# The second half of x arrives transposed; TensorE spreads the inverse roots

## The chip, the cores and the metric

One core of a Trainium2 chip runs the kernel. The metric is the time of one execution on the device in microseconds (us), as the median of several runs. A profile of one execution shows where the time goes. TensorE multiplies matrices into PSUM, VectorE and ScalarE work on SBUF and PSUM, GpSimd (POOL) on SBUF, and SyncE (SP) issues the DMAs.

## The reference

One layer of a streaming encoder, for a prompt of 2048 frames and 64 further frames of a running stream, with D = 1024:

```python
def rmsnorm(x, g=None):
    y = xf * lax.rsqrt(jnp.mean(xf * xf, axis=-1, keepdims=True) + EPS)
    return y * g

h = rmsnorm(x, norm_g) @ w_in
qa, ka, va, za, qb, kb, vb, zb, ga, gb = jnp.split(h, _split_points(), axis=-1)
# branch A: differential attention on qa, ka, va; branch B: retention on qb, kb, vb
m = ga * (oa @ w_oa) + gb * (ob @ w_ob)
return x + m @ w_out
```

What is changed concerns the first step alone: x is normalised frame by frame (one inverse root for each frame, one gain norm_g for each of the 1024 channels), and the product with w_in needs it with the channels on the partitions.

## The kernel before

**Precision.** A product in fp32 is made of three fast ones: each operand is split into a high part (rounded to fp32r) and a low part (the rest), and hi·hi, hi·lo and lo·hi are added up in PSUM. So x is kept as `xh` and `xl`, the weights as `wh` and `wl`. Every 128-channel chunk of a product is three matmuls (`mm_group`, L484 to L501; the matmuls are L493).

**Two halves.** The 2048 frames are worked off in two halves of 1024, the 64 sample frames with the first. `xh` and `xl` hold one half, in two segments of 512 frames (the second with 64 more in the first half). For each half all columns of w_in pass by, in blocks: va, ka, qa (frames on the output's partitions, `natural`, L576, with the finishes `fin_va` L685 and `fin_qk` L605), later qb, kb, za, zb, ga, gb (`transposed`, L738, with `fin_t` L754). The last block of the first half is the second part of gb. When its last product with a segment has been issued, that segment is free (`seg_free`, L751), and the second half's frames are put into it.

**How the second half of x is made.** When the first half is at its last block, `x_prep(1)` (L254) begins to load eight tiles of 128 frames into buffers of the tag `row`, eight of 128x1024 that attention shares. `x_norm` (L352) makes each tile's inverse root: squares with their sum on ScalarE (L321), log and exponential there (L323, L324), a correction on VectorE (L330 to L338); then VectorE scales the tile by the root and by the gain, which was broadcast over the partitions by a DMA (L347, `gn`). `x_tile` (L364) then transposes the tile on TensorE, four 128x128 blocks into one bank of PSUM (`tp`) and four into another (`pv`), both L376; ScalarE copies a bank to `xh` (L383), and VectorE takes the difference to `xl` (L384).

**What comes next.** The first block of the second half is va again, in groups of two tiles: 48 matmuls of 128x256. Its finish `fin_va` copies the result on ScalarE to `thi` (L698) and to `raw` (L700) and takes the rest on VectorE to `tlo` (L702), and three DMAs store them.

**What sets the order.** The code is a set of generators with priorities. A loop (L86) runs the one with the best priority that can go on, and keeps a clock of its own for each engine, moved by assumed costs (`P`, `A`, `V`, `G`, `ld`, L119 to L139). A generator that must wait yields the time at which it wants to go on. So the order in which each engine gets its instructions is worked out when the program is built; on the chip every engine runs its list in that order and waits on semaphores. The loop decides what stands ahead of what in a list, and not when it runs. All DMAs go through SP's list.

## Time and profile before

| | |
|---|---|
| median of 3 runs | 2009.26 us (2008.01 to 2015.51) |
| the profiled execution's own time | 2009.56 us |
| its span, first to last instruction | 2007.8 us |
| mean granted TensorE clock | 0.997 |
| GpSimd waiting for ScalarE's weight copies (wl L465 <- wh L455) | 620.2 us in total |
| TensorE's longest wait for another engine | 3.0 us |

Lines of the profile read as follows. In the order of time: start, duration, engine, line, operation, output<-inputs, shape, count, and in brackets the idle time ahead of it with what ended it. In the groups: busy time of the group and the mean duration of one in ns, then idle time ahead of its instructions. PE is TensorE, DVE VectorE, ACT ScalarE, SPq the DMA issues of SP. Matmuls overlap in the pipeline, so the step from one start to the next, and not the duration, is the time that one takes in a stream. In a table by stretches each engine has its busy time, PEclk is the granted clock (1.00 is full speed).

### The profile page before, as it was taken

What the parts mean: (1) busy time and instruction counts of PE and PEld (TensorE: products, weight loads), DVE (VectorE), ACT (ScalarE), POOL (GpSimd) and SP (SyncE); (2) the same over time, 40 slices, a digit from 0 to 9 for tenths busy, and PEclk for the clock granted to TensorE, in tenths of its full rate; (3) what the DMA queues carried; (4) which work ended last, traced back from release to release, by engine and by line L of the source; (5) the groups of instructions that cost most, each with busy time, mean ns of one, the idle gap of its engine ahead of it and who ended that gap; (6) DMA issues with size and microseconds to landing.
All of it is one profiled execution on the core that took longest, in us unless ns stands there. A gap on an engine that the chain in (4) does not pass through costs nothing. (4 is left out here: it accounts for less than half of the span.)

```text
span 2007.8 us, 34354 instructions
## 1 busy us (share of the span) xinstructions
PE 1988.0 (99%) x12412; PEld 1784.0 (89%) x12412; DVE 991.3 (49%) x2661; ACT 955.6 (48%) x2096; POOL 420.3 (21%) x387
## 2 busy tenths in 40 slices
PE   9999999999999999999999999999999989999999
PEld 7778999999998999999999888888888878889997
DVE  5452666553331421446856555635653365444442
ACT  6432776654442433536665656635654553333320
POOL 2310211211111212221211111122112442222210
PEclk9999999999999999999999999999999999999999
DMA  7647454344565563563352352553234674444431
GB/s 247 199 145 178 135 157 123 109 141 141 157 169 130 146 185 92 180 200 111 117 160 80 91 154 66 142 171 95 64 97 128 197 224 153 149 140 138 137 94 59
DMA packets 330268, 280.96 MB, mean 140 GB/s; under 512 B 64689, under 2 KB 296113, under 8 KB 330098
## 3 DMA queue, kind: packets, MB, share of 16 engines
q1 hardware_dynamic: 330098, 278.77, 47.1%
q8 instruction: 98, 1.61, 0.3%
q14 instruction: 72, 0.59, 0.1%
HBM read 187.19 MB, written 91.49 MB: 139 GB/s over the span
## 5 line engine op out<-in xcount | busy, mean ns | idle before, releaser
L493 PE MATMUL mm<-xh,wh 128*128 128x512 f32 (+2 forms) x1280 | 461.2, 360 | 0.0
L493 PE MATMUL mm<-xh,wl 128*128 128x512 f32 (+2 forms) x1280 | 451.7, 353 | 0.0
L493 PE MATMUL mm<-xl,wh 128*128 128x512 f32 (+2 forms) x1280 | 450.9, 352 | 0.0
L465 POOL TENSOR_TENSOR wl<-ws,wh 128x512 fp32r<-128x512 f32 x189 | 250.8, 1339 | 903.6 <-ACT wh L455 620.2
L493 PE MATMUL mm<-wh,xh 128*128 128x256 f32 (+3 forms) x864 | 272.0, 315 | 0.3 <-DVE tlo L702 0.3
L493 PEld LDWEIGHTS mm<-xh,wl 128*128 128x128 f32 x1280 | 240.9, 188 | 32.0
L493 PEld LDWEIGHTS mm<-xh,wh 128*128 128x128 f32 x1280 | 241.2, 188 | 29.6 <-issue 0.2
L493 PEld LDWEIGHTS mm<-xl,wh 128*128 128x128 f32 x1280 | 241.4, 189 | 29.1
L493 PE MATMUL mm<-wh,xl 128*128 128x256 f32 (+3 forms) x864 | 267.0, 309 | 0.1
L493 PE MATMUL mm<-wl,xh 128*128 128x256 f32 (+3 forms) x864 | 266.6, 309 | 0.0
L759 ACT COPY ev<-mm 128x512 f32<-128x512 f32 x140 | 71.6, 511 | 242.0 <-PE mm L493 217.8
L493 PEld LDWEIGHTS mm<-wh,xh 128*128 128x128 f32 (+1 forms) x864 | 162.2, 188 | 11.4 <-ACT xh L383 0.5
L493 PEld LDWEIGHTS mm<-wl,xh 128*128 128x128 f32 (+1 forms) x864 | 162.4, 188 | 10.6
L493 PEld LDWEIGHTS mm<-wh,xl 128*128 128x128 f32 (+1 forms) x864 | 162.2, 188 | 10.7 <-DVE xl L384 0.8
L1055 DVE TENSOR_TENSOR atl<-at,ath 128x512 fp32r<-128x512 f32 (+1 forms) x144 | 93.8, 660 | 139.9 <-ACT ath L1053 139.8
L972 ACT ACTIVATE row<-row,a_mx 128x1024 f32<-128x1024 f32 (+7 forms) x160 | 153.5, 962 | 16.8 <-DVE a_mx L952 16.7
L942 DVE CUSTOM_DVE_ANT_0 row<-s,dfar 128x512 f32<-128x512 f32 (+2 forms) x192 | 117.9, 632 | 74.8 <-PE s L934 73.6
L455 ACT CAST wh<-ws 128x512 fp32r<-128x512 f32 x192 | 116.5, 618 | 41.4 <-PE mm L493 28.0
L1053 ACT CAST ath<-at 128x512 fp32r<-128x512 f32 (+1 forms) x144 | 79.6, 563 | 99.2 <-PE at L1040 96.7
L933 PE MATMUL s<-K,q 128*128 128x512 f32 (+3 forms) x320 | 120.3, 381 | 2.5 <-DVE a_acc L942 2.5
L934 PE MATMUL s<-K,q 128*128 128x512 f32 (+3 forms) x320 | 115.5, 362 | 0.8 <-DMA q<-qT 0.8
L993 DVE SCALAR_TENSOR_TENSOR row<-row,a_w 128x1024 f32<-128x1024 f32 (+4 forms) x96 | 98.1, 1032 | 26.7 <-ACT row L990 26.4
(208 smaller groups left out, 3943.1 us busy)
## 6 DMA issues: line engine op xcount, KB each, us to landing
ws<-in_w_in_dram SPq DMA_DIRECT2D x192, 256.0 KB, 3.1
q<-qT SPq DMA_DIRECT2D x128, 128.0 KB, 3.0
V<-vN SPq DMA_DIRECT2D x24, 512.0 KB, 5.2
K<-kT SPq DMA_DIRECT2D x48, 256.0 KB, 4.4
gt<-gaT SPq DMA_DIRECT2D x64, 132.0 KB, 2.1
gt<-gbT SPq DMA_DIRECT2D x64, 132.0 KB, 2.2
xt<-in_x_prompt_dram SPq DMA_DIRECT2D x16, 512.0 KB, 6.0
kn<-in_cache_k_T_dram SPq DMA_DIRECT2D x32, 256.0 KB, 3.6
```

The costliest lines, as they stand in the source:

```text
L455: self.nc.scalar.copy(h, st)
L465: self.nc.gpsimd.tensor_sub(l, st, h.bitcast(F32))
L493: nc.tensor.matmul(ps, p, q, start=c == 0 and i == 0, stop=c == KC - 1 and i == 2)
L759: nc.scalar.copy(ev, ps)
L933: nc.tensor.matmul(ps, q1s, kk, start=True, stop=False)
L934: nc.tensor.matmul(ps, q2s, kk, start=False, stop=True)
L942: nc.vector.tensor_tensor_reduce(out=units[k0 // 1024][:, k0 % 1024:k0 % 1024 + n], in0=ps, in1=tab, scale=-SLOPES[h], scalar=3.0e38, op0= ...
L972: nc.scalar.activation(u, u, AF.Exp, bias=mx, scale=-1.0, accum_out=lp[:, k:k + 1])
L993: nc.vector.scalar_tensor_tensor(out=u0, in0=u0, scalar=w[:, 0:1], in1=u1, op0=ALU.mult, op1=ALU.add)
L1053: nc.scalar.copy(ah[:, :w], at[:, :w])
L1055: nc.vector.tensor_sub(al[:, :w], at[:, :w], ah[:, :w].bitcast(F32))
```

## The change

The host hands in `x_prompt` a second time, transposed. The kernel loads the second half of x in four pairs of tiles (256 frames): as before, to get the roots, and transposed, as two buffers of 4 chunks x 256 frames. The tiles themselves are no longer transposed. Each tile's 128 roots are put on the diagonal of a 128x128 matrix (`dg`, VectorE), and TensorE multiplies a matrix of ones (1/128; the root is multiplied by 128) by it: every partition then has all roots of the frames in PSUM. VectorE multiplies the transposed frames, chunk by chunk, by this and by the gain of the channel, which now lies on the partition (`gT`, a small load at the start). ScalarE copies the result to `xh`, VectorE takes the difference to `xl`, 1024 columns at a time. The first half of x is made as before.

```diff
+        self.gT = c("gT", [128, 8])
+        self.ld(self.gT, i["norm_g"][0].rearrange("(c p) -> p c", p=128))
...
+    def xt_load(self):
+        yield from self.take("row", 2)
+        jk, dg = self.row("xjk"), self.row("dg")
+        for p in range(4):
+            t0 = 1024 + 256 * p
+            dp = dg[:, 256 * p:256 * p + 256]
+            for u in range(2):
+                yield from self.take("row")
+                xt = self.row("xt")
+                t = self.ld(xt, self.i["x_prompt"][0, t0 + 128 * u:t0 + 128 * u + 128, :], 1 << 19)
+                self.spawn(self.xt_root(xt, jk, dp[:, 128 * u:128 * u + 128], t, p), 1, "w")
+            yield from self.take("row", 2)
+            xT = [self.row("xT") for _ in range(2)]
+            for k in range(2):
+                t = self.ld(xT[k].rearrange("p (c t) -> p c t", c=4),
+                            self.i["x_prompt_T"][512 * k:512 * k + 512, t0:t0 + 256]
+                            .rearrange("(c p) t -> p c t", p=128), 1 << 19)
+            self.xin.append([xT, t, dp, []])
+            yield self.pe
...
+    def xt_root(self, xt, jk, dg, t, p):
...
+        nc.vector.tensor_scalar(dg, self.ident, y, None, op0=ALU.mult)
...
+    def xt_pairs(self):
+        for p in range(4):
+            seg, col = p // 2, 256 * (p % 2)
...
+            rb = self.psum("tp")[:, :256]
+            for u in range(2):
+                nc.tensor.matmul(rb[:, 128 * u:128 * u + 128], self.ones, dp[:, 128 * u:128 * u + 128],
+                                 start=True, stop=True)
...
+            for k in range(2):
+                for c in range(4):
+                    xc = xT[k][:, 256 * c:256 * c + 256]
+                    nc.vector.scalar_tensor_tensor(out=xc, in0=xc, scalar=self.gT[:, 4 * k + c:4 * k + c + 1],
+                                                   in1=rb, op0=ALU.mult, op1=ALU.mult)
...
+            for k in range(2):
...
+                nc.scalar.copy(hi, xk)
+                t2 = self.A(1024, t)
+                yield t2
+                nc.vector.tensor_sub(lo, xk, hi.bitcast(F32))
+                t2 = self.V(1024, t2)
+                self.give("row", t2)
+            self.xt_ready += [t2, t2]
...
-                    self.spawn(self.x_prep(1), 1, "w")
-                    self.xt_ready = []
-                    self.spawn(self.x_tiles(8), 2, "w")
+                    self.xt_ready, self.xin = [], []
+                    self.spawn(self.xt_load(), 1, "w")
+                    self.spawn(self.xt_pairs(), 2, "w")
...
+    given["x_prompt_T"] = np.ascontiguousarray(given["x_prompt"][0].T)
```

More of the change, by code (lines that the diff above doesn't have):

```diff
@@ L39 @@
 QUANT = 6
-XFLY = (3, 5)
+XFLY = 3
 EARLY = 3
@@ L252, in x_alloc, with x_prep @@
         self.xl[seg] = xp.tile([128, KC, n], F32R, tag=f"xl{seg}", name=f"xl{seg}")
-    def x_prep(self, half):
+    def x_prep(self):
         self.xq = []
@@ L257, in x_prep @@
         self.xfly = 0
-        gn = jk = tg = None
-        if half:
-            yield from self.take("row", 2)
-            gn, jk = self.row("gn"), self.row("xjk")
-        else:
-            yield from self.take("row")
-            jk = self.row("xjk")
-        tiles = self.xtiles(half)
+        gn = tg = None
+        yield from self.take("row")
+        jk = self.row("xjk")
+        tiles = self.xtiles(0)
         left = [len(tiles)]
         for j, (src, r, seg, col) in enumerate(tiles):
-            yield lambda: self.xfly < XFLY[half] and (half > 0 or j < 2 or self.wloads >= 8)
+            yield lambda: self.xfly < XFLY and (j < 2 or self.wloads >= 8)
             self.xfly += 1
@@ L273, in x_prep @@
             tx = self.ld(xt, src, 4096 * r)
-            if j == 0 and half == 0:
+            if j == 0:
                 yield from self.take("row")
@@ L282, in x_prep @@
                 self.gz = (gz, tg)
-            elif j == 0:
-                tg = self.ld(gn, self.i["norm_g"][0].partition_broadcast(128), 1 << 19)
             self.xin.append([xt, jk, gn, tx, tg, r, seg, col, left])
-            if half:
-                self.spawn(self.x_norm(j), 1, "w")
             yield self.pe
         yield lambda: left[0] == 0
-        if half == 0:
-            self.give("s", self.dve + LAT, 2)
-        self.give("row", self.dve + LAT, 1 + half)
+        self.give("s", self.dve + LAT, 2)
@@ new lines, in x_prep @@
+        self.give("row", self.dve + LAT)
+    def xt_load(self):
+        nc = self.nc
+        yield from self.take("row", 2)
[3 more added lines that the diff above has]
+            dp = dg[:, 256 * p:256 * p + 256]
+            td = 0.0
+            for u in range(2):
+                yield from self.take("row")
+                xt = self.row("xt")
[9 more added lines that the diff above has]
+            yield self.pe
+        yield lambda: len(self.xt_ready) == 8
+        self.give("row", self.pe + LAT, 2)
@@ new lines, in xt_root @@
+    def xt_root(self, xt, jk, dg, t, p):
+        nc = self.nc
+        yield t
+        st = self.sp.tile([128, 3], F32, tag="x_st", name="x_st")
+        ss, ms, y = (st[:, k:k + 1] for k in range(3))
+        nc.scalar.activation(jk, xt, AF.Square, accum_out=ss)
+        t = self.A(1024, self.pe, 190)
+        self.give("row", t)
+        nc.scalar.activation(y, ss, AF.Ln, scale=1.0 / D, bias=self.epst)
+        nc.scalar.activation(y, y, AF.Exp, scale=-0.5)
+        self.A(1, 0, 40)
+        t2 = self.A(1, 0, 40)
+        yield t
+        nc.vector.tensor_scalar(ms, ss, 1.0 / D, EPS, op0=ALU.mult, op1=ALU.add)
+        self.V(1, t)
+        yield t2
+        nc.vector.tensor_scalar(ms, y, y, ms, op0=ALU.mult, op1=ALU.mult)
+        nc.vector.tensor_scalar(ms, ms, -0.5, 1.5, op0=ALU.mult, op1=ALU.add)
+        nc.vector.tensor_scalar(y, y, ms, 128.0, op0=ALU.mult, op1=ALU.mult)
+        nc.vector.tensor_scalar(dg, self.ident, y, None, op0=ALU.mult)
+        for _ in range(4):
+            t = self.V(40, t2)
+        self.xin[p][3].append(t)
@@ new lines, in xt_pairs @@
+    def xt_pairs(self):
+        nc = self.nc
+        for p in range(4):
+            seg, col = p // 2, 256 * (p % 2)
+            yield lambda: len(self.xin) > p and len(self.xin[p][3]) == 2
+            xT, tx, dp, ts = self.xin[p]
+            yield max(ts)
+            yield from self.take("tp")
+            rb = self.psum("tp")[:, :256]
+            for u in range(2):
+                nc.tensor.matmul(rb[:, 128 * u:128 * u + 128], self.ones, dp[:, 128 * u:128 * u + 128],
+                                 start=True, stop=True)
+                t = self.P(512)
+            if max(t, tx) > self.pe:
+                yield max(t, tx)
+            for k in range(2):
[3 more added lines that the diff above has]
+                                                   in1=rb, op0=ALU.mult, op1=ALU.mult)
+                    t = self.V(256, t)
+            self.give("tp", t)
+            if p % 2 == 0:
+                yield lambda: self.seg_free[seg] is not None
+                yield self.seg_free[seg]
+                self.seg_free[seg] = None
+                self.x_alloc(seg)
+            if t > self.pe:
+                yield t
+            for k in range(2):
+                hi = self.xh[seg][:, 4 * k:4 * k + 4, col:col + 256]
+                lo = self.xl[seg][:, 4 * k:4 * k + 4, col:col + 256]
+                xk = xT[k].rearrange("p (c t) -> p c t", c=4)
+                nc.scalar.copy(hi, xk)
+                t2 = self.A(1024, t)
+                yield t2
+                nc.vector.tensor_sub(lo, xk, hi.bitcast(F32))
+                t2 = self.V(1024, t2)
+                self.give("row", t2)
+            self.xt_ready += [t2, t2]
@@ L337, in norm_root @@
         nc.vector.tensor_scalar(ms, ms, -0.5, 1.5, op0=ALU.mult, op1=ALU.add)
-        nc.vector.tensor_scalar(y, y, ms, 128.0 if isinstance(self.xin[j][2], list) else 1.0,
-                                op0=ALU.mult, op1=ALU.mult)
+        nc.vector.tensor_scalar(y, y, ms, 128.0, op0=ALU.mult, op1=ALU.mult)
         for _ in range(3):
@@ L344, in norm_scale @@
         xt, jk, gn, tx, tg, r, seg, col, left, ss, ms, y, t, t2 = self.xin[j]
-        for k, g in enumerate(gn if isinstance(gn, list) else [gn]):
-            sl = slice(512 * k, 512 * k + g.shape[1])
+        for k, g in enumerate(gn):
+            sl = slice(512 * k, 512 * k + 512)
             self.nc.vector.scalar_tensor_tensor(out=xt[:, sl], in0=xt[:, sl], scalar=y, in1=g[:r],
@@ L350, in norm_scale, with x_tile @@
         left[0] -= 1
-    def x_norm(self, j):
-        yield self.xin[j][3]
-        self.norm_sums(j)
-        ss, ms, y, t, t2 = self.xin[j][9:]
-        yield t
-        self.norm_mean(j)
-        yield t2
-        self.norm_root(j)
-        if self.xin[0][4] > self.pe:
-            yield self.xin[0][4]
-        self.norm_scale(j)
-    def x_tile(self, j, wait=True):
+    def x_tile(self, j):
         nc = self.nc
-        yield lambda: len(self.xq) > j and self.xq[j] is not None
         xt, t, r, seg, col = self.xq[j]
-        if wait:
-            yield t
         self.until(t)
@@ L389, in x_tile @@
         self.xt_ready.append(t2)
-    def x_tiles(self, n):
-        for j in range(n):
-            if j == 0 or j == 4:
-                yield lambda: self.seg_free[j // 4] is not None
-                yield self.seg_free[j // 4]
-                self.seg_free[j // 4] = None
-                self.x_alloc(j // 4)
-            yield from self.x_tile(j)
     def w_load(self):
@@ L522, in opening @@
         self.norm_root(1)
-        yield from self.x_tile(0, False)
+        yield from self.x_tile(0)
         self.norm_scale(1)
@@ L533, in opening @@
             if k == "T":
-                yield from self.x_tile(1, False)
+                yield from self.x_tile(1)
                 self.norm_sums(2)
@@ L562, in between @@
                         self.norm_root(j + 2)
-                    yield from self.x_tile(j + 1, False)
+                    yield from self.x_tile(j + 1)
                     if j + 2 < 9:
@@ L1687, in w_stream @@
         self.wloads = 0
-        self.spawn(self.x_prep(0), 0, "w")
+        self.spawn(self.x_prep(), 0, "w")
         self.spawn(self.w_load(), 0, "w")
```

## The prediction

> **What bounds the kernel now.** I read the page's busy shares first, then the table by stretches, then who waited for whom on TensorE, and last the instructions in order of time around the place that the change touches.

> ```profile
> span 2007.8 us, 34354 instructions
> PE 1988.0 (99%) x12412; PEld 1784.0 (89%) x12412; DVE 991.3 (49%) x2661; ACT 955.6 (48%) x2096; POOL 420.3 (21%) x387
> ...
> core 0: us, PE busy (x) PEld busy (x) DVE busy (x) ACT busy (x) POOL busy (x), PEclk, DMA share, GB/s
> 20.00:40.00 20.00, 20.00 (x101) 16.69 (x101) 12.16 (x28) 9.49 (x22) 0.00 (x0) 1.00 0.69 214
> 785.00:838.00 53.00, 53.00 (x399) 51.15 (x398) 28.41 (x59) 31.32 (x69) 10.10 (x8) 1.00 0.47 139
> 1626.00:1660.00 34.00, 27.91 (x150) 24.12 (x149) 31.99 (x63) 21.98 (x54) 20.18 (x21) 0.85 0.78 243
> ```

> TensorE is the bound: 99% of the span. The change works between 785 and 838 us, where the first half of x gives way to the second. There TensorE has no idle time at all (53.00 of 53.00), at full clock, so what is taken from its stream shortens the run by as much, and a wait put into it lengthens the run by as much. No attention work is in the stream there to fill a wait: its next task needs keys that this stretch has yet to make.

> **The change part by part.** *Removed: 64 transposes.* They stand in the stream like this:

> ```profile
> start us, us, engine line op out<-in xcount [idle before <-releaser]
> 801.85 0.28 PE L493 MATMUL mm<-xh,wh 128*128 128x256 f32 x1
> 801.97 0.28 PE L493 MATMUL mm<-xl,wh 128*128 128x256 f32 x1
> ...
> 802.57 0.60 PE L376 MATMUL tp<-ident,xt 128*128 128x128 f32 x4
> 803.00 0.60 PE L376 MATMUL pv<-ident,xt 128*128 128x128 f32 x4
> 803.36 0.36 PE L493 MATMUL mm<-xh,wh 128*128 128x256 f32 x1
> 803.56 0.28 PE L493 MATMUL mm<-xl,wh 128*128 128x256 f32 x1
> ...
> L376 PE MATMUL tp<-ident,xt 128*128 128x128 f32 x64 | 9.6, 272 | 0.0
> ```

> What counts is the step from start to start, since matmuls overlap. A 128x256 matmul steps by 0.12 us. Two groups of four transposes hold the stream from 802.57 to 803.36, 0.79 us, and the matmul behind them steps 0.20 instead of 0.12: 0.87 us for two groups, 0.43 for one. The second half has 8 tiles x 2 groups: 16 x 0.43 = **6.9 us removed**. [...]

> *Added on TensorE: 8 fp32 matmuls of 128x128, ones by dg, in four pairs (a "spread" each).* The nearest row is the fp32 matmul of L801, 256 columns wide, recorded as two passes:

> ```profile
> 219.63 0.28 PE L493 MATMUL mm<-wh,xl 128*128 128x256 f32 x1
> 219.75 0.59 PE L801 MATMUL tp<-r_sq,ones 128*128 128x256 f32 x2
> 219.99 0.58 PE L933 MATMUL s<-K,q 128*128 128x512 f32 x1
> 220.41 0.40 PE L934 MATMUL s<-K,q 128*128 128x512 f32 x1
> 220.65 0.28 PE L933 MATMUL s<-K,q 128*128 128x256 f32 x1
> ```

> From 219.75 to 220.41 are 0.66 us, of which a 128x512 step is 0.23 or 0.24 (220.41 to 220.65): 0.43 for 256 columns, thus 0.43 for a pair of 128 columns and 4 x 0.43 = **1.7 us added**. Bounds: 0.36 (the stream price of four transposes) to 0.87 a pair, 1.4 to 3.5 in all. TensorE's own account is -6.9 + 1.7 = -5.2 us.

> *Moved: how xh and xl of a segment come about.* Before, each 128-frame tile was split from PSUM in two halves of 512 columns. Now a pair of tiles (256 frames) is scaled in place by VectorE (8 instructions of 128x256), then ScalarE copies 1024 columns to xh, VectorE subtracts 1024 columns to xl, and both do so a second time for the other four chunks. The rows for the durations:

> ```profile
> L321 ACT ACTIVATE xjk<-xt 128x1024 f32<-128x1024 f32 x16 | 17.0, 1064 | 3.5 <-DMA xt<-in_x_prompt_dram 3.5
> L347 DVE SCALAR_TENSOR_TENSOR xt<-xt,x_st,gn 128x1024 f32<-128x1024 f32 x8 | 10.3, 1285 | 0.4
> L1137 DVE TENSOR_TENSOR atl<-kn,ath 128x512 fp32r<-128x512 f32 x32 | 25.4, 794 | 14.5 <-ACT ath L1135 14.5
> L811 DVE SCALAR_TENSOR_TENSOR r_sq<-tp,r_sq 128x256 f32<-128x256 f32 x33 | 13.7, 415 | 8.1 <-ACT r_sq L806 8.0
> ...
> 802.05 0.59 ACT L759 COPY ev<-mm 128x512 f32<-128x512 f32 x1 [1.36 <-PE mm L493]
> ...
> 818.08 0.59 ACT L698 CAST thi<-mm 128x512 fp32r<-128x512 f32 x1
> 818.56 0.59 ACT L700 COPY raw<-mm 128x512 f32<-128x512 f32 x1
> 819.04 0.60 ACT L383 CAST xh<-pv 128x512 fp32r<-128x512 f32 x1
> ...
> 820.65 0.69 DVE L702 TENSOR_TENSOR tlo<-mm,thi 128x512 fp32r<-128x512 f32 x1
> 821.25 0.14 DVE L330 TENSOR_SCALAR x_st<-x_st 128x1 f32<-128x1 f32 x1
> ```

> ScalarE begins 0.20 us after a group's last step (801.85 to 802.05), and its instructions of 512 columns follow each other every 0.48 us. A copy of 1024 columns I take at 1.06 (L321; at most two 512s, 1.2), a subtraction of 1024 from SBUF at 1.29 (L347; at most two of L1137, 1.6), the low ends, since one long instruction saves a start. Scaling a pair is 8 x 0.42 = 3.4 us at most (L811).

> The orders of ScalarE and VectorE are fixed at build time and decide the rest. The first product of the second half works by pairs too: two tiles x 24 matmuls x 0.12 = 5.7 us a group, and then its finish: thi and raw on ScalarE, tlo on VectorE (0.69, the next starts 0.60 after it, 820.65 to 821.25).

> Pair 0 is hidden. Its scaling precedes the release of segment 0. From that release to its first use TensorE has 24 steps of 128x256, 24 of 128x320 and a spread, 2.9 + 3.5 + 0.4 = 6.8 us. Needed: 0.20 + 0.48 (the copy of ev ahead) + 1.06 + 1.29 + 1.2 = 4.2 us. Without that cover it would cost these 4.2.

> Pair 1 is not hidden. In VectorE's order both its subtractions stand behind the tlo of the first group, and tlo waits for that group's end. After the end: 0.20 + 0.59 (thi) + 0.05 + 0.60 (tlo) + 1.29 = 2.7 us until xl is there. TensorE can only do pair 2's spread (0.43) and the two matmuls on xh (0.24): **a stop of 2.1 us**.

> Pairs 2 and 3: here the xh copies also stand behind thi and raw of the previous group in ScalarE's order: 0.20 + 0.48 + 0.48 + 1.06 + 0.05 + 1.29 = 3.6 us after that group's end, less 0.24, and less 0.43 where a spread is left (pair 2): **2.9 and 3.3 us**. The second half of each pair comes 1.2 us after the first, and the first four chunks occupy TensorE 1.4 us. The stops make 8.3 us, up to 10 with the high durations (three subtractions x 0.3, two copies x 0.14, one tlo wait more), and down to 0 if TensorE found them done.

> So far -5.2 + 8.3 = **+3.1 us**.

> *The clock.* The stops are long enough to matter here:

> ```profile
> 1630.54 0.28 PE L1547 MATMUL s<-ogh,w_o_retl 128*128 128x264 f32 x1
> 1633.83 0.39 PE L1545 MATMUL mm<-ogh,w_o_diffh 128*128 128x264 f32 x1 [3.01 <-DVE gt L1565]
> 1634.30 0.38 PE L1545 MATMUL mm<-ogh,w_o_diffh 128*128 128x264 f32 x1
> 1634.70 0.42 PE L1547 MATMUL mm<-ogh,w_o_diffl 128*128 128x264 f32 x1
> 1634.92 0.42 PE L1545 MATMUL mm<-ogh,w_o_diffh 128*128 128x264 f32 x1
> ...
> 1637.77 0.29 PE L1546 MATMUL s<-ogl,w_o_reth 128*128 128x264 f32 x1
> ...
> 1652.51 0.80 PE L1614 MATMUL at<-woh,ml 128*128 128x512 f32 x1 [2.42 <-DVE ml L1583]
> 1653.53 0.63 PE L1613 MATMUL at<-wol,mh 128*128 128x512 f32 x1
> ```

> After an idle time of 3.01 us the steps are 0.22 instead of 0.12 from 1634.30 to 1637.77, and after 2.42 us they are slow again; the granted clock of 1626 to 1660 is 0.85. The first slow spell is 3.4 us at half rate, 1.7 us lost; the second goes from 1652.51 to about 1658, 2.5 us lost. Two of my three stops are of that size, so I count two drops x 1.7 = **+3.4 us**; bounds 0 and three x 2.5 = 7.5. [...]

> *What hides the rest.*

> ```profile
> L136 SPq DMA_DIRECT2D bg<-in_b_gate_dram x1: 432/432/432, 25.1 to 25.1; - x1
> ...
> xt<-in_x_prompt_dram SPq DMA_DIRECT2D x16, 512.0 KB, 6.0
> ```

> On SP, one load of gT (its like, bg, took 0.43 us to issue) and eight of xT come in, one of gn goes: TensorE is busy throughout both stretches. Pair 2's and pair 3's xT wait for rows that the subtractions of pairs 0 and 1 set free; at 6.0 us to landing (the row of xt) they are there 2 us or more before VectorE turns to them. The root chains and dg are VectorE work of about 1 us a tile in its idle half (28.41 of 53). TensorE's order outside this stretch is the same in both kernels, so nothing else should move.

> **Sum.** -6.9 + 1.7 + 8.3 + 3.4 = +6.5 us on the profiled execution's 2009.56, its span 2007.8 and 1.8 around it: 2016.1. It lies 0.3 above the median of the runs shown, so I predict a median of **2015.8 us**, +0.3%.

> **The rivals.**
> [...]
> 2. *Slower by more than 0.5%: the clock drops at each stop.* Place: the three group ends. Price: 2.5 us each, as after 1652.51, so -5.2 + 8.3 + 7.5 = +10.6, a median of 2019.9. It decides if a stop of 2.1 us already drops the clock; the 2.42 us row speaks for it, the shorter stop of pair 1 against.
> 3. *Faster: the stops do not appear.* If the finish of a group did not hold up the next pair, only TensorE's account is left: -5.2, 2004.1. For: VectorE and ScalarE are about half idle in the stretch. Against: the queues are in order, and idle time behind a waiting instruction is of no use.
> 4. *The stream price of transposes is not won*, because the spreads cost 0.87 a pair: +1.8 on the forecast, within its range.

> **How the numbers follow.** Forecast (2013.5 to 2019.2) 0.50; rival 1 0.20; rival 2 0.20; rival 3 0.06; rival 4 or something else 0.04. A measurement of this kernel can tell about 0.5%, 10 us, from no change: 1999.2 to 2019.3. Rival 2 lies above that, rival 3 inside it: faster 0.02, within 0.78, slower 0.20. The range must take in rival 1 and the middle of rival 2: 2009 to 2021.

> **What would show it.** In the profile after: 64 fewer L376 transposes between 785 and 845 and four pairs of tp<-dg,ones at about 0.43 us each. Idle time of TensorE ahead of matmuls that read xl and xh, three stops of about 2.1, 2.9 and 3.3 us, put down to VectorE's xl; TensorE less than fully busy there, about 8 us in all; a granted clock under 1 in that stretch. ScalarE's xh copies of pairs 2 and 3 beginning right behind a raw copy. I am wrong in the main step if TensorE has no idle time there, wrong in the clock if the steps stay at 0.12, and wrong in the bounds if TensorE's time outside this stretch changes by over 2 us.

## The result, and the profile after

The changed kernel takes 2019.34 us (median of 6 runs, 2018.70 to 2021.67) beside 2009.44 us before (6 runs). The ratio is 1.0047, with a 95% interval of 1.0037 to 1.0057: **slower by 9.9 us, 7.4 to 11.5 by the interval**. The forecast was 2015.8, that is +6.5. The profiled execution took 2018.76 us, its span is 2017.0 against 2007.8.

The head of the page after, the table by stretches (first the kernel before from 785 to 845 us, then the changed one from 785 to 838 and to 845), and TensorE's waits in the stretch:

```profile
span 2017.0 us, 34294 instructions
PE 1989.0 (99%) x12364; PEld 1781.7 (88%) x12364; DVE 997.6 (49%) x2685; ACT 954.1 (47%) x2088; POOL 418.6 (21%) x387
```

```profile
785.00:845.00 60.00, 60.00 (x457) 58.15 (x456) 29.40 (x61) 33.75 (x73) 13.98 (x11) 1.00 0.50 148
```

```profile
785.00:838.00 53.00, 45.79 (x305) 42.38 (x303) 32.70 (x82) 28.49 (x58) 8.04 (x7) 0.97 0.65 202
785.00:845.00 60.00, 52.34 (x349) 48.93 (x348) 34.23 (x83) 29.82 (x60) 9.02 (x8) 0.94 0.59 184
```

```profile
PE mm L552 <- DVE xl L373: 4.4, 4, 2.3
...
PE mm L552 <- ACT xh L370: 2.5, 2, 2.1
...
PE tp L347 <- DVE dg L331: 0.7, 1, 0.7
```

TensorE has 48 instructions fewer (64 transposes less 8 spreads recorded as 16). In the stretch where it had no idle time it now has 60.00 - 52.34 = 7.66 us, and the clock there is 0.94. The three waits add up to 7.6 us (in each line: us in total, times, the longest), and all three sit in this stretch. Here they are in TensorE's order of time:

```profile
814.77 0.60 PE L347 MATMUL tp<-dg,ones 128*128 128x128 f32 x4
815.14 0.36 PE L552 MATMUL mm<-wh,xh 128*128 128x256 f32 x1
815.34 0.28 PE L552 MATMUL mm<-wl,xh 128*128 128x256 f32 x1
817.96 0.39 PE L552 MATMUL mm<-wh,xl 128*128 128x256 f32 x1 [2.34 <-DVE xl L373]
818.18 0.28 PE L552 MATMUL mm<-wh,xh 128*128 128x256 f32 x1
...
820.19 0.39 PE L552 MATMUL mm<-wh,xl 128*128 128x256 f32 x1 [0.54 <-DVE xl L373]
...
824.62 0.46 PE L347 MATMUL tp<-dg,ones 128*128 128x128 f32 x2
825.73 0.49 PE L347 MATMUL tp<-dg,ones 128*128 128x128 f32 x2 [0.65 <-DVE dg L331]
826.63 0.39 PE L552 MATMUL mm<-wh,xh 128*128 128x256 f32 x1 [0.42 <-ACT xh L370]
827.89 0.58 PE L552 MATMUL mm<-wh,xl 128*128 128x256 f32 x1 [0.76 <-DVE xl L373]
828.27 0.41 PE L552 MATMUL mm<-wh,xh 128*128 128x256 f32 x1
828.48 0.41 PE L552 MATMUL mm<-wl,xh 128*128 128x256 f32 x1
...
831.22 0.28 PE L552 MATMUL mm<-wh,xl 128*128 128x256 f32 x1
...
837.19 0.39 PE L552 MATMUL mm<-wh,xh 128*128 128x256 f32 x1 [2.11 <-ACT xh L370]
838.45 0.58 PE L552 MATMUL mm<-wh,xl 128*128 128x256 f32 x1 [0.75 <-DVE xl L373]
...
841.39 0.29 PE L552 MATMUL mm<-wh,xh 128*128 128x256 f32 x1
```

Three stops, one for each of the pairs 1, 2 and 3. A restart costs more than its bracket: from 815.34 to 817.96 are 2.62 us where a step is 0.12, thus 2.50 lost for 2.34 of idle time, and the next step is 0.22, 0.10 more; 0.26 a restart in all. Pair 2's stop has four late starts: three with a bracket, and the first half of pair 3's spread (824.62), which starts 0.25 us later than the step of 0.12 would have it, without a bracket. So pair 1 lost 2.88 + 2 x 0.26 = 3.4 us, pair 2 1.83 + 4 x 0.26 = 2.9, pair 3 2.86 + 2 x 0.26 = 3.4, together **9.7**. The late spread adds nothing of its own: the matmul behind it waits for the copy to xh, which began at 825.52, right behind raw. Behind the stops of pairs 2 and 3 the steps are 0.21 instead of 0.12, and the granted clock is 0.50 (827.89 to 831.04, 838.45 to 841.18): from 827.89 to 831.22 3.33 us for 15 steps, from 838.45 to 841.39 2.94 us for 13, which without the restarts lose 1.4 and 1.3, together **2.7**. With -6.9 for the transposes and +1.8 for the spreads this makes +7.3.

To see where the whole 9.2 us of span arose, take the same ScalarE instructions in both kernels, ahead of and behind the stretch, and at both ends of a late one. Before:

```profile
784.77 0.43 ACT L759 COPY ev<-mm 128x320 f32<-128x320 f32 x1 [0.41 <-PE mm L493]
846.23 0.21 ACT L229 ACTIVATE sm_y<-ms 128x8 f32<-128x8 f32 x1 [1.56 <-DVE ms L637]
1115.50 0.59 ACT L759 COPY ev<-mm 128x512 f32<-128x512 f32 x1 [1.42 <-PE mm L493]
1541.56 0.59 ACT L759 COPY ev<-mm 128x512 f32<-128x512 f32 x1 [1.02 <-PE mm L493]
```

After:

```profile
784.66 0.43 ACT L818 COPY ev<-mm 128x320 f32<-128x320 f32 x1 [0.41 <-PE mm L552]
853.47 0.21 ACT L231 ACTIVATE sm_y<-ms 128x8 f32<-128x8 f32 x1 [1.56 <-DVE ms L696]
1123.29 0.59 ACT L818 COPY ev<-mm 128x512 f32<-128x512 f32 x1 [1.41 <-PE mm L552]
1550.32 0.59 ACT L818 COPY ev<-mm 128x512 f32<-128x512 f32 x1 [1.02 <-PE mm L552]
```

**The stretch** took 61.46 us before and 68.81 after: +7.35, as the account above has it. **The late stretch** took 426.06 and 427.03: +0.97, though TensorE's instructions there are the same in the same order. The remaining 0.9 of the span is -0.11 ahead of the stretch, +0.55 between the two (+0.50 in run 11) and +0.44 behind the late one; it is not explained. In run 8, which only adds gT, these three parts differ from the kernel before by +3.91, -0.09 and -1.7.

### The profile page after: what moved, and what is told of

It is laid out like the page before. It is cut to its first block, busy times and chain, and to the rows that moved or that the text cites. A ratio compares the mean times of both kernels' runs of the same rounds, so it can differ in the third digit from the quotient of the medians.

```text
span 2017.0 us, 34294 instructions
## 1 busy us (share of the span) xinstructions
PE 1989.0 (99%) x12364; PEld 1781.7 (88%) x12364; DVE 997.6 (49%) x2685; ACT 954.1 (47%) x2088; POOL 418.6 (21%) x387
## 4 chain that ended last, share of the span: by engine, by line
PE 93%; DVE 3%; ACT 1%; DMA 1%; issue 1%; SPq 0%; DVEq 0%; ACTq 0%
PE mm L552 52%; PE s L992 3%; PE s L993 3%; PE at L1671 3%; PE at L1673 3%; PE at L1099 3%; PE at L1672 3%; PE pv L1078 2%; PE pv L1079 2%; PE pv L1077 2%; PE pv L1276 1%; PE mm L1604 1%; PE mm L1606 1%; PE mm L1605 1%; PE s L1605 1%; PE s L1606 1%
## 6 DMA issues: line engine op xcount, KB each, us to landing
V<-vN SPq DMA_DIRECT2D x24, 512.0 KB, 5.3
xt<-in_x_prompt_dram SPq DMA_DIRECT2D x16, 512.0 KB, 5.7
```

## The experiments

Theory A: the orders of ScalarE's and VectorE's lists make the stops, and the stops bring the half clock. Theory B: the preparation of a pair takes that long wherever it stands. The table gives for each kernel the ratio to the kernel before, what the two stretches above gained against it, read at the same instructions, and TensorE's idle time between 785 and 845 us where it was read.

| run | edit | ratio (95%) | stretch, us | late, us | idle, us |
|---|---|---|---|---|---|
| after | the change | 1.0047 (1.0037 to 1.0057) | +7.35 | +0.97 | 7.66 |
| 1 | pairs 1, 2 ahead of the finish | 1.0023 (1.0014 to 1.0031) | +2.14 | +0.98 | 4.42 |
| 2 | all pairs ahead | 1.0007 (0.9999 to 1.0016) | -0.54 | +0.97 | 3.23 |
| 3 | stops filled with matmuls | 1.0029 (1.0018 to 1.0040) | +4.64 | +0.98 | 3.03 |
| 4 | before, transposes twice | 1.0032 (1.0020 to 1.0044) | +7.07 | 0.00 | 0.00 |
| 5 | one group ahead, pieces of 512 | 1.0027 (1.0017 to 1.0037) | +2.38 | +0.97 | 4.48 |
| 6 | pieces of 512 | 1.0046 (1.0031 to 1.0061) | +3.73 | +0.95 | 5.62 |
| 7 | tlo ahead of raw | 1.0072 (1.0055 to 1.0089) | +9.30 | +0.98 | |
| 8 | before, with gT | 1.0009 (1.0000 to 1.0017) | +0.08 | +0.98 | |
| 9 | before, gT of 64 bytes | 0.9993 (0.9984 to 1.0002) | +0.06 | -0.68 | |
| 10 | two pairs scaled first, 64 bytes | 1.0018 (1.0009 to 1.0027) | +6.61 | -0.64 | 6.50 |
| 11 | after, gT of 64 bytes | 1.0032 (1.0020 to 1.0045) | +7.31 | -0.66 | 7.66 |
| 12 | as 10, loads in the old order | 1.0022 (1.0013 to 1.0031) | +4.73 | -0.64 | 5.98 |

**Run 1: undo the wait between copy and subtraction.**

```diff
                 t2 = self.A(1024, t)
-                yield t2
                 nc.vector.tensor_sub(lo, xk, hi.bitcast(F32))
```

The loop now emits pairs 1 and 2 ahead of the finish of the group before; pair 3 stays behind one.

> The xh copies and xl subtractions of pairs 1 and 2 now stand ahead of the finish (thi, raw, tlo) of the group before them in the lists of ScalarE and VectorE; those of pair 3 still stand behind a finish. Theory A (the order of the lists makes the stops, and the stops bring the half clock): pair 1's stop of 3.4 us goes, pair 2's falls from 3.1 to about 1, pair 3's of 3.5 stays, and one of the two half-clock spells (1.4 us lost each) goes: 2019.3 - 3.4 - 2.1 - 1.4, about 2012.5 us. Theory B (the preparation of a pair takes that long wherever it stands, by its own durations or by its DMA): the stops stay in sum, 2019.3 us.

The kernel took 4.5 us more than the kernel before (2015.00 beside 2010.51). Its waits for xh and xl:

```profile
PE mm L551 <- ACT xh L370: 2.1, 1, 2.1
PE mm L551 <- DVE xl L372: 1.8, 2, 1.1
```

Pair 1's stop is gone, pair 2's is one wait of 1.1, pair 3's is as it was (2.1 and 0.7), and one of the two half-clock spells is left (steps of 0.21 from 835.56 on). The stretch fell by 5.2 us where theory A had 6.9 and theory B nothing. The order makes the stops of pairs 1 and 2.

**Run 2: the same, and copies right behind the scaling.**

```diff
-            if t > self.pe:
-                yield t
             for k in range(2):
...
-                yield t2
```

> As the run before, and also the copies and subtractions follow right behind a pair's scaling: pairs 0, 1 and 2 are prepared ahead of the first group's tlo, pair 3 ahead of the third group's finish. Theory A: no stop of over 0.5 us, no half clock in the stretch, so only TensorE's own account (-6.9 + 1.7) is left against the kernel before: 2019.3 - 10.0 - 2.7, 2006.6 us, or 2004.2 if the 2 us lost outside the stretch were only the scatter of one profile. Theory B (durations or DMA, not order): stops of about 10 us in sum stay, 2019 us.

The kernel took 1.8 us more than the kernel before (2012.30 beside 2010.51). There is no half clock in the stretch (the profiled execution's mean clock is 0.998, the changed kernel's 0.995), and the stretch is 0.54 us shorter than before. The old stops are gone but for 0.67 us. What theory A had not foreseen are new ones. TensorE, then ScalarE:

```profile
812.83 0.39 PE L549 MATMUL mm<-wh,xh 128*128 128x256 f32 x1 [1.67 <-ACT ev L815]
814.97 0.39 PE L549 MATMUL mm<-wl,xh 128*128 128x256 f32 x1 [0.32 <-POOL wl L521]
```

```profile
811.46 1.05 ACT L368 CAST xh<-xT 128x1024 fp32r<-128x1024 f32 x1 [0.51 <-DVE xT L355]
812.41 0.36 ACT L815 COPY ev<-mm 128x256 f32<-128x256 f32 x1
```

Pair 1's copies now wait for VectorE's scaling in front of `ev`, which frees TensorE's next PSUM buffer, and in front of a weight copy, from which GpSimd makes wl. A preparation put too early holds up the finish of an earlier block, as a finish put too early holds up the preparation.

**Run 3: the clock.** 8, 6 and 8 matmuls of ones by ones are put in front of the groups of pairs 1, 2 and 3, their result unused:

```diff
+                    if u == 0 and j0:
+                        dm = self.psum("at")
+                        for _ in range(6 if j0 == 4 else 8):
+                            self.nc.tensor.matmul(dm[:, 0:128], self.ones, self.ones, start=True, stop=True)
```

> The changed kernel with 8, 6 and 8 further matmuls (ones by ones, 128 columns, fp32, result unused, 0.22 us each) in front of the groups of pairs 1, 2 and 3; the lists of the other engines are unchanged, so the data come no earlier and TensorE only waits less idly. Theory A (idle time brings the half clock): no half-clock steps behind the stops, -2.7 us, 2016.6 us. Rival (the slow steps behind the stops have another cause than TensorE's idle time, for instance operands that still arrive late): unchanged, 2019.3 us, or above if the added work outlasts the stops.

The stretch falls from +7.35 to +4.64, by 2.71 us; the time goes from 9.9 to 6.4 us above the kernel before (2016.91 beside 2010.51). The data come no earlier (pair 1's xl is taken at 818.18 against 817.96, and the spread ahead of its group began 0.23 later already, at 815.00 against 814.77), but the clock holds. The stretch:

```profile
785.00:845.00 60.00, 56.97 (x414) 53.73 (x413) 34.92 (x84) 31.64 (x63) 11.74 (x10) 1.00 0.61 188
```

Its clock is 1.00, the last column but two, where the changed kernel had 0.94. With 3.03 us of idle time in place of 7.66 the half clock did not come; here it had cost 2.7 us.

**Run 4: the price of the transposes.** The kernel before issues each transpose of the second half twice:

```diff
-                nc.tensor.transpose(tp[:, c * r:(c + 1) * r],
+                for _ in range(2 if wait else 1):
+                    nc.tensor.transpose(tp[:, c * r:(c + 1) * r],
```

> The kernel before with each of the 64 transposes of the second half issued twice into the same place, nothing else changed: it measures what 64 transposes cost in the stream. By the steps from start to start (0.43 us for four): +6.9 us, 2016.3 us against 2009.4. By the mean duration of 272 ns: 64 x 0.272 = +17.4, 2026.8 us.

The stretch grew by 7.07 us, the median by 6.7 (2017.18 beside 2010.51). The forecast's 6.9 us for 64 transposes is right, and the mean duration of 272 ns, 17.4 us, is excluded by the interval (4.0 to 8.8).

**Run 6: shorter pieces.** Copies and subtractions of 512 columns, in the order of the changed kernel:

```diff
+                for s in (slice(0, 2), slice(2, 4)):
+                    nc.scalar.copy(hi[:, s], xk[:, s])
+                    t2 = self.A(512, t)
+                    yield t2
+                    nc.vector.tensor_sub(lo[:, s], xk[:, s], hi[:, s].bitcast(F32))
```

> The changed kernel with the same order against the finishes, but with each copy and subtraction in two pieces of 512 columns, so that the first matmuls can begin after a copy of 0.6 and a subtraction of 0.7 instead of 1.06 and 1.2. Theory A: the first wait of each stop is shorter by 0.5 (pair 1, subtraction alone) and 1.0 us (pairs 2 and 3, copy and subtraction), 2.5 in sum, if the later pieces keep up; the time falls to 2016.8 or a little less, where a half-clock spell goes too. Rival (length of the pieces does not count, since the whole pair has to be there before the group can go on): 2019.3.

The profiled execution's stretch is 3.6 us shorter than the changed kernel's, but the median is not: it is 2019.36 in 5 runs from 2015.15 to 2021.91, 9.5 above the kernel before (2009.84). The profiled execution was the shortest of the five, with a granted clock of 0.998; the others had 0.994 to 0.997. So the waits are shorter in the profile, and a gain in time is not shown.

**Run 7: why pair 1's stop was longer than forecast.** The changed kernel's lists around it, ScalarE, VectorE and GpSimd:

```profile
814.97 0.59 ACT L757 CAST thi<-mm 128x512 fp32r<-128x512 f32 x1 [1.99 <-PE mm L552]
815.45 0.59 ACT L759 COPY raw<-mm 128x512 f32<-128x512 f32 x1
...
816.08 0.69 DVE L761 TENSOR_TENSOR tlo<-mm,thi 128x512 fp32r<-128x512 f32 x1 [2.92 <-ACT raw L759]
816.69 3.44 DVE L373 TENSOR_TENSOR xl<-xT,xh 128x1024 fp32r<-128x1024 f32 x2
...
817.59 1.46 POOL L524 TENSOR_TENSOR wl<-ws,wh 128x512 fp32r<-128x512 f32 x1 [4.51 <-ACT wh L514]
```

`tlo` began when `raw` ended (815.45 + 0.59 = 816.04), not when `thi` did. And two subtractions took 3.44 us: the first some 1.2, the second until 820.13, that is 1.1 us behind the end of GpSimd's `wl` at 819.05. The edit puts `tlo` ahead of `raw`:

```diff
-            nc.scalar.copy(raw, ps)
-            t2 = self.A(n, t)
             nc.vector.tensor_sub(lo, ps, hi.bitcast(F32))
             t3 = self.V(n, t1)
+            nc.scalar.copy(raw, ps)
+            t2 = self.A(n, t)
```

> The changed kernel with the finish's tlo subtraction put ahead of the raw copy, so that it waits for thi alone. Two causes are proposed for pair 1's stop being 3.4 us and not 2.1: tlo waited for raw (0.45 us), and the second subtraction of the pair waited for GpSimd's wl, which had begun 0.9 us after the first subtraction and ended where the second began. If both hold, the first idle time falls from 2.34 to 1.9, the two subtractions take 2.4 in place of 3.44, as the first now ends before wl begins, and the idle time of 0.54 ahead of the second is gone: 1.0 to 1.5 us less in all, 2018. If tlo waited for something else: unchanged. Pairs 2 and 3 keep their stops, since there xh is copied behind raw.

ScalarE, then VectorE, at the same place:

```profile
821.60 0.59 ACT L761 COPY raw<-mm 128x512 f32<-128x512 f32 x1 [0.76 <-DVE tlo L759]
...
820.87 0.69 DVE L759 TENSOR_TENSOR tlo<-mm,thi 128x512 fp32r<-128x512 f32 x1 [2.43 <-ACT thi L757]
821.48 1.22 DVE L373 TENSOR_TENSOR xl<-xT,xh 128x1024 fp32r<-128x1024 f32 x1
823.16 1.23 DVE L373 TENSOR_TENSOR xl<-xT,xh 128x1024 fp32r<-128x1024 f32 x1 [0.47 <-ACT xh L370]
```

At pair 1 the figures are those of both causes: the first idle time is 1.85 instead of 2.34, and the subtractions take 1.22 and 1.23. But the expected time was wrong by far: the median is 2025.86 (beside 2009.84) instead of 2018. Now `raw` waits for `tlo` (821.56), and the xh copies of pairs 2 and 3, which stand behind `raw`, come later by as much. Pair 3's first wait went from 2.11 to 3.01 us. `fin_va` also serves the first half of x, and part of the loss lies there: the profiled execution is 3.8 us behind the changed kernel's by 78 us, where no profile of the other kernels is more than 2.3 us behind the kernel before. In this program the two readers of one PSUM tile go one after the other, in whichever order they are written: the second begins when the first has ended (816.08 after 816.04 in the changed kernel, 821.60 after 821.56 here).

**Runs 8, 9 and 11: the late stretch.** Run 8 adds to the kernel before only the constant gT (8 columns, 32 bytes on a partition) and its load, unused; run 9 makes it 64 bytes; run 11 does that to the changed kernel.

```diff
+        self.gT = c("gT", [128, 8])
+        self.ld(self.gT, i["norm_g"][0].rearrange("(c p) -> p c", p=128))
```

```diff
-        self.gT = c("gT", [128, 8])
-        self.ld(self.gT, i["norm_g"][0].rearrange("(c p) -> p c", p=128))
+        self.gT = c("gT", [128, 16])
+        self.ld(self.gT[:, :8], i["norm_g"][0].rearrange("(c p) -> p c", p=128))
```

> The kernel before with the small constant gT and its load added, and not used. All kernels with the change lost the same 0.96 us between 1116 and 1540 us, in small steps at the same places, with the same list of instructions there; the kernel before and its variant with doubled transposes lost nothing there. If the constant in front of the other buffers does it (it moves the addresses of all that come after it), the loss of about 1 us appears here; if it is how the second half is prepared (the buffers of xh, xl and the rows), the stretch stays as before, to 0.1 us, and the time is that of the kernel before.

> As the run with gT added alone to the kernel before, but the constant is 16 columns wide (64 bytes on each partition) instead of 8 (32 bytes), so that everything behind it moves by 64 bytes; the load is the same. If the slower steps between 1116 and 1540 us (0.98 us in that run) come from where the buffers lie, in steps of 64 bytes, they vanish and the time is that of the kernel before; if the further load or any shift at all does it, they stay, about 2 us above the kernel before.

> The changed kernel with gT 64 bytes wide instead of 32 and nothing else. If the shift of all later buffers is a term of its own, next to the stops, it shows here as it did without the rest of the change: the steps between 1116 and 1540 us go from +0.96 to about -0.65 us against the kernel before, the stops and the two half-clock spells stay, and the time falls from 9.9 to about 8 us above the kernel before. If the shift counts only beside the old order: unchanged, 9.9 above.

The ends of the late stretch in run 8, then in run 9:

```profile
1119.40 0.59 ACT L761 COPY ev<-mm 128x512 f32<-128x512 f32 x1 [1.41 <-PE mm L495]
1546.44 0.59 ACT L761 COPY ev<-mm 128x512 f32<-128x512 f32 x1 [1.01 <-PE mm L495]
```

```profile
1113.41 0.59 ACT L761 COPY ev<-mm 128x512 f32<-128x512 f32 x1 [1.41 <-PE mm L495]
1538.79 0.59 ACT L761 COPY ev<-mm 128x512 f32<-128x512 f32 x1 [1.01 <-PE mm L495]
```

427.04 us with 32 bytes, 425.38 with 64, 426.06 without the constant. All eight kernels with 32 bytes lost 0.95 to 0.98 us here, all four with 64 bytes gained 0.64 to 0.68. So the width of a constant that nothing there uses, not the change of the algorithm, makes this term. The medians of runs 8 and 9 are 2.3 us above and 1.0 below the kernel before, both at the edge of their intervals, so the term is read from the stretch alone. In run 11 the stops and the stretch stayed (+7.31) and the time went to 6.8 us above the kernel before (2016.07 beside 2009.29). The term gives 1.6 us of this fall from 9.9; the rest is inside the two intervals, which overlap. That the addresses behind the constant do it is the likely reading, since the load is the same; the addresses themselves were not varied in finer steps.

**Runs 5, 10 and 12: an order that would beat both.** Run 5 keeps the waits for pairs 0 and 1 only and cuts the pieces:

```diff
-            if t > self.pe:
+            if p < 2 and t > self.pe:
                 yield t
...
-                yield t2
...
+                for s in range(0, 4, 2):
+                    nc.scalar.copy(hi[:, s:s + 2], xk[:, s:s + 2])
...
+                    nc.vector.tensor_sub(lo[:, s:s + 2], xk[:, s:s + 2], hi[:, s:s + 2].bitcast(F32))
```

> The changed kernel with each pair's copies and subtractions one whole group ahead of their use in both lists, and behind the last block's ev and weight copies, which the second run had got in the way of; pieces of 512 columns in place of 1024. Theory A: no stop above 0.7 us and no half clock in the stretch; the stretch gives about -5.2 + 0.5 against the kernel before, and about 1 us of slower steps between 1116 and 1540 us stays, as in every kernel so far that had the change: 3.7 us under the kernel before of the same call. Theory B (the work of preparing a pair, not its place, is too much for the stretch): stops come back elsewhere, as in the second run, and the time is at or above the kernel before.

The kernel took 5.8 us more than the kernel before (2015.64 beside 2009.84). The stops of pairs 1 and 2 are gone; pair 3's are worse (0.71 and 0.64 ahead of its spread, then 1.61 and 1.51), as its roots stand behind the second group's `tlo`. Run 10 scales pair 1 before the copies of pair 0, loads the tiles for the roots of pairs 2 and 3 ahead, and gives pairs 2 and 3 out without a modelled wait; run 12 goes back to the old order of loads and drops the modelled waits of pair 3 alone. Both split the work on a pair into a scaling and a putting in place:

```diff
+        yield from self.xt_scale(0)
         for p in range(4):
+            if p == 0:
+                yield from self.xt_scale(1)
+            elif p > 1:
+                yield from self.xt_scale(p)
+            yield from self.xt_put(p)
```

> The change in an order that takes in what the runs showed: pair 1 is scaled before the copies of pair 0, the tiles for the roots of pairs 2 and 3 are loaded ahead of their transposed frames, pair 2 is prepared wholly ahead of the first group's tlo, pair 3 ahead of the second group's thi; no copy stands in front of an ev or a weight copy that is due earlier; gT is 64 bytes wide. Theory A (order and place explain the loss): stops under 0.7 us in sum, no half clock in the stretch, -5.2 + 0.7 there; with the slower steps outside gone 4 us under the kernel before, with them left 2 to 3 us under. Theory B (the stretch has no room on VectorE and ScalarE for this preparation): stops of 3 us or more are left, as in the second and fifth runs, and the time is at or above the kernel before.

> As the tenth run (pair 1 scaled ahead of pair 0's copies, 64 bytes for gT), but the loads keep the order of the changed kernel, so that pair 2's transposed frames come ahead of pair 3's tiles, and pair 3's roots are not held behind a modelled time. In the tenth run pair 2's second buffer landed late (VectorE idle 1.91 us between its two scalings), which held ScalarE's copies, the first group's thi and tlo behind them, and so pair 3's dg: 3.9 us of TensorE. If that chain was the cause, the 3.9 us go to under 1, the 2.0 us that TensorE waited for GpSimd's weights behind four subtractions in a row stay, the stretch gives -5.2 + 2.5, and the time is about 3 us under the kernel before. If VectorE and ScalarE have no room for the preparation, a stop of 3 us or more turns up elsewhere and the time is at or above the kernel before.

Run 10 took 4.2 us more than the kernel before (2013.75 beside 2009.55), run 12 4.7 (2013.98 beside 2009.29). Both have two half-clock spells in the stretch, where theory A had none; their clocks between 785 and 845 us are 0.91 and 0.94. Run 10's TensorE, VectorE and GpSimd:

```profile
825.95 0.46 PE L356 MATMUL tp<-dg,ones 128*128 128x128 f32 x2 [3.90 <-DVE x_st L326]
...
805.75 4.63 DVE L385 TENSOR_TENSOR xl<-xT,xh 128x1024 fp32r<-128x1024 f32 x4
...
819.91 1.66 DVE L364 SCALAR_TENSOR_TENSOR xT<-xT,gT,tp 128x256 f32<-128x256 f32 x4 [1.91 <-issue]
...
807.79 6.19 POOL L536 TENSOR_TENSOR wl<-ws,wh 128x512 fp32r<-128x512 f32 x3 [10.30 <-ACT wh L526]
```

The three stops of the changed kernel are gone, and one of 3.9 us stands ahead of pair 3's spread, besides 2.0 us for weights that GpSimd made late while VectorE subtracted four times in a row. Run 12, with the loads in the old order, has VectorE's 1.91 us away and still 3.3 us ahead of that spread: there pair 3's squares stand behind the first group's `raw` on ScalarE. The last pair of run 12, from its spread to its last subtractions:

```profile
825.37 0.80 PE L357 MATMUL tp<-dg,ones 128*128 128x128 f32 x2 [0.70 <-DVE dg L333]
...
829.35 2.42 DVE L386 TENSOR_TENSOR xl<-xT,xh 128x1024 fp32r<-128x1024 f32 x2
```

From 825.37 to 831.77 are 6.4 us, more than the 5.8 of a group on TensorE, and the roots come ahead of it. This is how long one pair takes from end to end; it forces a stop only if the pair is begun no earlier than the group ahead of it. So theory A holds for the stops of the changed kernel, and theory B in part for the other orders: each one tried moved the wait to another link of this chain. No order of the change beat the kernel before; run 2 comes nearest (by its interval from 0.2 us faster to 3.2 slower). That no order could is not shown.

## Why the prediction was right, and where its sizes were off

- **The account of TensorE** (-6.9, +1.7) holds: run 4 gives 7.07 for the transposes, and a spread takes 0.45 (814.77 to 815.14, and 0.08 more in the step behind it), 1.8 in all. Rival 4 falls.
- **Pair 0 hidden**: yes, no wait at its first use.
- **The stops**: all three came where forecast. Of the 7.66 us of idle time 6.9 are put down to xl and xh, and 0.65 to pair 3's dg, in the shadow of the wait for xh. In price, pair 2 took 2.9 (2.9 forecast) and pair 3 3.4 (3.3). The mis-sized term is **pair 1**: 3.4 instead of 2.1. Its step "0.20 + 0.59 (thi) + 0.05 + 0.60 (tlo) + 1.29" left out that tlo also waits for raw (0.5) and that the second subtraction is held up beside GpSimd's wl (2.3 us instead of 1.2, thus 1.1 late; 0.54 of it TensorE waits out, and 0.26 is its restart). Rival 3 falls; runs 1 and 2 show that the order of the lists is the cause.
- **The clock**: there were two drops, behind pairs 2 and 3, as forecast. They cost 2.7 us instead of 3.4, since each spell lost 1.4 or 1.3 and not 1.7; 1.7 takes a spell at half rate, while the forecast's own row has steps of 0.22 for 0.12, by which 3.4 us lose 1.5. That the clock holds (rival 1) and that it drops at each stop (rival 2) both fall, and run 3 measures the same 2.7.
- **What starts a drop** is not shown. The length of one gap does not decide it: pair 1's 2.34 us brought no drop (the steps are 0.12 from 818.18 on), while the longest gap ahead of the first drop is 0.76 us, with 0.65 and 0.42 shortly before. The forecast had named pairs 2 and 3 because their stops would be the longer ones; in the trace pair 1's stop (2.88 us idle) is as long as pair 3's (2.86) and longer than pair 2's (1.83). So two drops at the named places came out, but not for the forecast's reason: this part is luck. Run 6's five executions of one program have mean clocks of 0.994 to 0.998, so the time at the half clock differs between executions.
- **"Nothing else should move"** failed: 0.97 us come from the constant gT, which the forecast had priced by its load alone (0.43 us, hidden). The load is hidden (run 9 has it too and lies 1.0 us below the kernel before); what the constant's width does to the late stretch is not.
- **The sum**: forecast -6.9 + 1.7 + 8.3 + 3.4 = +6.5; in the trace -6.9 + 1.8 + 9.7 + 2.7 = +7.3 (7.35 measured) and 0.97 late, 8.3 of the span's 9.2. The rest up to the medians' 9.9 is within the interval and not assigned. Two errors in the sum partly cancel: +1.3 at pair 1 and -0.7 at the clock.
- **The time alone would have misled**: 2019.34 lies just above the forecast's own band (2013.5 to 2019.2) and next to rival 2's 2019.9. Only the trace tells them apart: two drops of 1.4 and 1.3 us, where rival 2 has three of 2.5. The range (2009 to 2021) held because it was drawn to take in the middle of rival 2.

## What to carry to other kernels

Where queues are fixed at build time, walk through each queue at the joint between two phases and ask what stands ahead of the new operand's preparation: removed TensorE work was worth 5.1 us here, and the finishes in front of three pairs' copies and subtractions, with the half clock that followed, took back 12.4. Each cure by order alone that was tried moved the wait to the next link, so add up the whole chain of one pair against the time of one group first. Before explaining a last microsecond by the algorithm, add the new constant alone to the old kernel.

## What the runs showed of the hardware that was not expected

```profile
811.97 1.18 DVE L331 TENSOR_SCALAR dg<-ident,x_st 128x128 f32<-128x128 f32 x1
...
811.78 1.30 POOL L524 TENSOR_TENSOR wl<-ws,wh 128x512 fp32r<-128x512 f32 x1 [2.42 <-ACT wh L514]
```

  With both operands in SBUF, VectorE's dg took 1.18 us instead of the 0.29 of the other seven when GpSimd's wl had begun 0.2 us before it; dg ended at 813.15, just behind wl at 813.08. Scalings and tlo, which read PSUM, kept their time beside wl: eight scalings took 3.22 us beside it (from 806.58) and 3.21 without it (from 820.05), tlo 0.69 beside it (846.66) and without it (816.08). The other way round, GpSimd took 6.19 us for three wl in run 10 beside VectorE's four subtractions, and 3.80 for three in the changed kernel from 844.03 on. What decides who is held up is open: wl is recorded as begun 0.23 us ahead of a subtraction both in the changed kernel (817.59 and 817.82), where the subtraction came late, and in run 10 (807.79 and 808.02), where wl did.
- A constant of 32 or 64 bytes in front of the other buffers moved 426 us of unchanged work by +0.97 or -0.66 us; why is open.
- In this program two engines that read the same PSUM tile go one after the other by a semaphore: tlo behind raw (816.08 after 816.04), and raw behind tlo when the order is turned (821.60 after 821.56). No run here lets them read at the same time.
